# Attention queries with features on partitions, and three smaller moves, in a one-core hybrid mLSTM and window-attention layer

## The chip, the cores and the metric

One Trainium2 chip, one core. The metric is the device time of one execution in microseconds. Before the change three runs took 2311.09, 2317.71 and 2320.4 us; the median is 2317.71 us.

## The reference

One layer of a streaming encoder, in fp32, for a prompt of 2048 tokens and a batch of 8 samples with 16 new tokens each (128 tokens). Model width 1024.

```
z  = x @ w_in                      # mLSTM q,k,v,output gate (4 heads x 128), gates, attention q (8x64), k,v (2x64)
hm = mlstm_chunkwise(q, k, v, ...) # matrix memory with a state per head
hm = sigmoid(o) * head_norm(hm)
qa, ka = rope(qa, pos), rope(ka, pos)
ha = window attention(qa, ka, va)  # own chunk of 64 and the two before it, a learned sink per head
x  = LayerNorm(alpha * x + concat(hm, ha) @ w_out)
u  = causal_depthwise_conv(x @ w_up)       # width 3, value | gate, 2 x 2816
y  = LayerNorm(alpha * x + (silu(gate) * value) @ w_down)
```

`rope` turns each head's two halves of 32 features by an angle that depends on the token: the first half becomes x1 cos - x2 sin, the second x2 cos + x1 sin. Results are y for all tokens, the mLSTM states, the last keys and values and the last rows before the convolution.

## The kernel before

Tokens are 17 tiles of 128: tiles 0 to 15 are the prompt, tile 16 the samples. There are three dense stages, all done as a Winograd form of Strassen's scheme with seven products (numbered 1 to 7) in place of eight: the input projection (blocks of four tiles in `IBLOCKS`, five column groups g of 512, `i_product`), the up-projection (`f_product`) and the down-projection (`f_downs`). The output projection (`o_block`, `group`) is plain. Every matmul operand is split into a high and a low fp32r part, and each product is three matmuls (high by high, high by low, low by high). `split` makes the parts: ScalarE casts the high one, VectorE subtracts to get the low one.

**Input projection.** `i_dense` goes through a written list of items. Groups 0 and 1 (mLSTM queries and keys) have the weights as stationary operand, so that features come out on partitions; groups 2, 3 and 4 (attention queries, output gate, values) have the tokens as stationary operand, so that tokens come out on partitions. `i_after` empties the three PSUM banks A, B, C after each product: ScalarE copies and VectorE adds, then `i_out` and `i_store` write the result to device memory. For group 2, `i_out` first applies `rope` (four VectorE operations on 128 x 512) and writes tokens x features to `zqa`.

**The two chains.** While the dense stages run, two generators work through the prompt's tiles: `m_chain` (mLSTM) and `a_chain` (window attention; `swa` is one tile). They start when `t_sample` has finished the samples. In `a_chain`, `swa_dma` loads the tile's queries and keys, `swa_load` transposes them on TensorE (four 128 x 128 transposes into the bank `pq`, one into `pk`), `swa_first` splits them. `swa` then computes scores in two halves, exponentials, divisions, transposes the weights and multiplies by the values, and `mix_out` writes the tile's result to `zmix`.

**The planner.** `Chains` interleaves them. TensorE's instructions run in the order in which they are written (a manual schedule); the other engines' order is set by the framework's scheduler from priorities. Each yield of a dense stage is worth 645 planned ns (six matmuls of 256 columns or three of 512); each yield of a chain gives its planned cost, the planned delay until its next step, and how many of the five PSUM banks must be free for it. `weave` lets a chain step in when its time has come and its banks are free by plan (`ask` holds each for 3500 ns or what `HOLDS` says). The step list is thus fixed when the program is written, from these numbers alone. `x_pair` loads the chains' results for the next block of the output projection: `OBLOCKS` are tiles 16, 0, 1; 2 to 5; 6 to 9; 10 to 13; 14 and 15, and in the last round of a block the next block's tiles are asked for with

```
for t in OBLOCKS[b]:
    self.chains.until(t)
```

`until` runs chain steps one after the other, with no dense step between, until the tile is ready.

**Weight sums.** The down-projection needs sums of weight blocks. `d_sums(k, step)` makes them during the last two input blocks and the output projection: step 0 loads two rows of `wdn` into `txy`, step 1 is four VectorE subtractions (L850 to L853), step 2 stores them to `zt`.

**End of the up-projection.** `f_evict` empties the banks; after product 5, ScalarE copies bank B to `ub` and VectorE adds bank C to it (L1906, L1908). In the last eight products of `f_ups`, `d_weights` and `d_tokens` prepare the down-projection's first operands with splits on ScalarE and VectorE.

**The end.** In `f_downs` the last product (3) of the last block is done column by column; the last tile's 512 columns are added (L2116), its statistics taken (L1559 and on), and `norm_last` normalises and stores it.

Of the kernel before, what the change touches and what calls it, by code (L numbers as in the profile page):

```python
# [14 lines left out]
P = 128  # L15
# [47 lines left out]
def _consts():  # L63
# [15 lines left out]
    c["rope"] = rp.reshape(NT, P, 3, half).transpose(1, 0, 2, 3)  # L79
    sel = np.zeros((36, MH), np.float32)  # L80
# [124 lines left out]
class Prog:  # L205
# [90 lines left out]
    def setup(self):  # L296
# [10 lines left out]
        self.zqa = [dp.tile([P, 512], F32, name=f"zqa{t}") for t in range(NT)]  # L307
# [384 lines left out]
    def i_product(self, b, g, s):  # L692
# [5 lines left out]
        for c in range(2):  # L698
            m = slice(c * P, c * P + P)
            o = ps[:, c * HT:(c + 1) * HT]  # L700
            for k in range(4):
                for i, (w, x) in enumerate(((wh, hh), (wh, hl), (wl, hh))):
                    l, r = (w[:, k, m], x[:, k]) if g < 2 else (x[:, k, m], w[:, k])
                    mm(o, l, r, start=s in (1, 7) and c == k == i == 0, stop=k == 3 and i == 2, skip_group_check=True)  # L704
# [38 lines left out]
    def i_store(self, b, g, i, j, ev):  # L743
# [3 lines left out]
        if g < 2:  # L747
            f = 4 * i + 2 * g
            nc.sync.dma_start(self.zqk[b][f:f + 2, :, j * HT:(j + 1) * HT].rearrange("f p m -> p f m"), v)
        else:  # L750
            z = (self.zqa, self.zog, self.zv)[g - 2]
# [3 lines left out]
    def i_out(self, b, g, i, j, src):  # L755
# [3 lines left out]
        if g == 3:  # L759
            nc.scalar.activation(ev, src, AF.Tanh, scale=0.5)  # L760
            nc.vector.tensor_scalar_add(ev, ev, 1.0)
        elif not i:
            nc.scalar.copy(ev, src)
        if g == 2:
            self.rope(ev, IBLOCKS[b][2 * j], 2)
        self.i_store(b, g, i, j, ev)

    def i_after(self, b, g, s):
# [4 lines left out]
        def add(u):  # L773
            if g < 2:
                V.scalar_tensor_tensor(u, C, KSCALE, u, op0=ALU.mult, op1=ALU.add)
            else:
                V.tensor_add(u, C, u)
# [23 lines left out]
    def i_batch(self, g):  # L801
# [5 lines left out]
        if g == 2:  # L807
            nc.scalar.copy(ev, ps)
            self.rope(ev, t, 1)
            nc.sync.dma_start(self.zqa[t], ev)  # L810
# [29 lines left out]
    def d_sums(self, k, step):  # L840
# [7 lines left out]
        if step == 1:  # L848
            l, r = slice(0, 512), slice(512, D)
# [8 lines left out]
    def rope(self, A, t, nt):  # L858
# [3 lines left out]
        B = self.mp.tile([P, 512], F32, name="rb", tag="rb", bufs=1)[:, :n]  # L862
# [366 lines left out]
    def swa_dma(self, t):  # L1229
        nc = self.nc  # L1230
        qa = self.work("qa", [P, 512])
        nc.sync.dma_start(qa, self.zqa[t])
        kv = self.work("kva", [P, 256], bufs=3)
        nc.sync.dma_start(kv, self.zkv[t])
        return qa, kv
# [24 lines left out]
    def swa_first(self, t):  # L1260
        nc = self.nc
        kv, pq, pk = self.swa_load(self.a_load)
        self.a_load = None
# [3 lines left out]
        qh, ql = self.work("qh", [P, 4, P], F32R), self.work("ql", [P, 4, P], F32R)  # L1267
        self.split(qh, ql, pq)
        self.split(self.kh[:, r], self.kl[:, r], pk)
        self.kv[r] = kv  # L1270
        self.a_first = qh, ql
# [918 lines left out]
```

## Time and profile before

| | |
|---|---|
| median of three runs | 2317.71 us |
| the profiled execution | 2321.38 us |
| its span, first to last instruction | 2319.6 us |
| mean granted TensorE clock | 0.995 |
| bytes moved by DMA | 632.39 MB, 273 GB/s |

The page gives each engine's busy time over the span, and what each group of instructions waited for. A row of the windows view names a stretch in us from the start of the span, its length, then busy time and instruction count of TensorE, its weight loads, VectorE, ScalarE and GpSimd (of one line alone where a line is asked for: then TensorE and its weight loads only), the granted TensorE clock, the mean busy share of the DMA engines, and GB/s. A row of the groups view gives line, engine, operation, operands, shape and count, then busy us and mean ns of one, then the idle time before. A row of the timeline gives start and length in us, and in brackets the idle time before it with what ended it.

### The profile page before, as it was taken

The numbers are of one execution on the slowest core, as the hardware profiler recorded it, in microseconds if no ns is written. First come the engines' busy times: TensorE is split into PE (matmuls) and PEld (weight loads), VectorE is DVE, ScalarE is ACT, GpSimd is POOL, SyncE is SP. The second block draws the span as 40 slices with busy tenths as digits, with TensorE's granted clock in tenths as the row PEclk, the third lists the DMA queues.
The fourth block names the chain that finished last, engine by engine and source line by source line (L and its number), as shares of the span: only waits on it lengthen the run. The fifth ranks groups of instructions, "written<-read, shape, count | busy, mean of one in ns | idle before, by whom it ended". The sixth has DMA issues, their size and how long they took to land. (4 is left out here: it accounts for less than half of the span.)

```text
span 2319.6 us, 39851 instructions
## 1 busy us (share of the span) xinstructions
PE 2287.3 (99%) x14293; PEld 2097.9 (90%) x14293; DVE 1818.9 (78%) x3189; ACT 1273.3 (55%) x2409; POOL 267.8 (12%) x477
## 2 busy tenths in 40 slices
PE   8999999999999999999999999999999999999998
PEld 8999989899977778999999999999999978888876
DVE  7777687787688888998788777678766786895987
ACT  5453466776766665555556555556555544444442
POOL 0001000100011112121102000003111200100200
PEclk9999999999999999999999999999999999999999
DMA  7888999989986767788777888888998776756743
GB/s 270 289 304 294 302 311 329 313 300 327 334 279 225 234 210 271 286 327 310 279 293 270 307 306 307 314 269 283 313 297 265 227 286 205 258 176 218 258 153 109
DMA packets 300166, 632.39 MB, mean 273 GB/s; under 512 B 47868, under 2 KB 141120, under 8 KB 299968
## 3 DMA queue, kind: packets, MB, share of 16 engines
q1 hardware_dynamic: 295296, 616.14, 77.5%
q0 software_dynamic: 3520, 10.56, 1.4%
q10 hardware_dynamic: 1152, 3.15, 0.4%
q8 instruction: 113, 1.85, 0.3%
q14 instruction: 85, 0.70, 0.1%
HBM read 458.11 MB, written 171.64 MB: 271 GB/s over the span
## 5 line engine op out<-in xcount | busy, mean ns | idle before, releaser
L1877 PE MATMUL dps<-hh,uw 128*128 128x384 f32 (+1 forms) x1848 | 478.1, 328 | 2.6 <-DVE u L1908 2.0
L1877 PE MATMUL fup<-hh,uw 128*128 128x384 f32 (+1 forms) x1848 | 478.1, 328 | 0.3 <-ACT ua L1898 0.2
L1877 PEld LDWEIGHTS dps<-hh,uw 128*128 128x128 f32 x1848 | 329.9, 188 | 3.1 <-DVE u L1908 2.3
L1877 PEld LDWEIGHTS fup<-hh,uw 128*128 128x128 f32 x1848 | 330.0, 188 | 0.8 <-ACT ua L1898 0.5
L1934 DVE SCALAR_TENSOR_TENSOR cc<-u,cw,cc 128x768 f32<-128x768 f32 (+1 forms) x264 | 258.2, 979 | 60.9 <-ACT cc L1932 51.8
L1877 PE MATMUL fup<-hl,uw 128*128 128x384 f32 (+1 forms) x924 | 302.5, 327 | 1.8 <-DVE hl L218 1.8
L1877 PE MATMUL dps<-hl,uw 128*128 128x384 f32 (+1 forms) x924 | 302.3, 327 | 0.0
L704 PE MATMUL dps<-w,oh 128*128 128x256 f32 x1344 | 254.9, 284 | 1.2 <-DMA w<-zws 0.7
L217 ACT CAST uw<-wraw 128x1024 fp32r<-128x1024 f32 x126 | 123.1, 979 | 222.8 <-PE dps L2087 120.1
L218 DVE TENSOR_TENSOR w<-wraw,w 128x1024 fp32r<-128x1024 f32 (+2 forms) x167 | 189.3, 1141 | 50.4 <-ACT w L217 45.7
L704 PEld LDWEIGHTS dps<-w,oh 128*128 128x128 f32 x1344 | 210.6, 188 | 12.7 <-issue 8.1
L217 ACT CAST w<-wraw 128x1024 fp32r<-128x1024 f32 (+2 forms) x167 | 163.2, 984 | 102.9 <-PE dps L704 37.3
L218 DVE TENSOR_TENSOR uw<-wraw,uw 128x1024 fp32r<-128x1024 f32 x126 | 142.5, 1132 | 64.3 <-ACT uw L217 64.3
L704 PE MATMUL dps<-w,ol 128*128 128x256 f32 x672 | 187.9, 280 | 0.0
L704 PE MATMUL dps<-oh,w 128*128 128x256 f32 x896 | 172.5, 287 | 6.2 <-ACT mr L1152 3.4
L1877 PEld LDWEIGHTS fup<-hl,uw 128*128 128x128 f32 x924 | 173.5, 188 | 2.5 <-DVE hl L218 2.4
L2087 PE MATMUL fup<-uw,fu 128*128 128x512 f32 x726 | 174.0, 396 | 0.6 <-DVE uw L218 0.6
L1877 PEld LDWEIGHTS dps<-hl,uw 128*128 128x128 f32 x924 | 173.5, 188 | 0.0
L2087 PEld LDWEIGHTS fup<-uw,fu 128*128 128x128 f32 x726 | 136.3, 188 | 34.0 <-DVE uw L218 1.1
L2087 PE MATMUL dps<-uw,fu 128*128 128x512 f32 x660 | 165.3, 396 | 1.1 <-DVE uw L218 1.1
L1932 ACT ACTIVATE cc<-u,cw 128x768 f32<-128x768 f32 (+1 forms) x132 | 132.2, 1001 | 52.6 <-DVE u L1914 26.7
L704 PEld LDWEIGHTS dps<-oh,w 128*128 128x128 f32 x896 | 143.5, 192 | 12.7 <-issue 4.1
(322 smaller groups left out, 4588.6 us busy)
## 6 DMA issues: line engine op xcount, KB each, us to landing
uw<-zw SPq DMA_DIRECT2D x176, 512.0 KB, 5.2
zw<-uw SPq DMA_DIRECT2D x88, 512.0 KB, 3.6
w<-zws SPq DMA_DIRECT2D x72, 512.0 KB, 6.4
wv<-wup SPq DMA_DIRECT2D x66, 512.0 KB, 4.8
wraw<-wi SPq DMA_DIRECT2D x65, 512.0 KB, 5.3
wraw<-zt SPq DMA_DIRECT2D x60, 512.0 KB, 4.3
wraw<-wdn SPq DMA_DIRECT2D x45, 512.0 KB, 4.2
wraw<-wo SPq DMA_DIRECT2D x40, 512.0 KB, 4.7
```

Of the source, the lines that this page charges most:

```text
L217: nc.scalar.copy(hi, src)
L218: nc.vector.tensor_sub(lo, src, hi.bitcast(F32))
L704: mm(o, l, r, start=s in (1, 7) and c == k == i == 0, stop=k == 3 and i == 2, skip_group_check=True)
L1877: mm(ps, l[:, k], r[:, k], start=s in (1, 7) and k == 0 and i == 0, stop=k == 3 and i == 2, skip_group_check=True)
L1932: S.activation(c[:, v], u[:, 2:2 + n], AF.Identity, bias=w[3], scale=w[2])
L1934: V.scalar_tensor_tensor(c[:, v], u[:, i:i + n], w[i], c[:, v], op0=ALU.mult, op1=ALU.add)
L2087: mm(ps, l[:, k, c], r[:, k], start=s in (1, 4, 7) and u == 0 and k == 0 and i == 0, stop=u == nu - 1 and k == n - 1 and i == 2, skip_grou ...
```

## The change

Four parts.

1. Group 2 of the input projection takes the weights as stationary operand too, so the prompt's queries come out with features on partitions and go to `zq[t]` without rotation. `swa_dma` loads a tile's queries (`qa`), a second copy with the two halves of 32 partitions swapped (`qb`, four DMAs of 32 partitions into the buffer of tag `ql`), and cosine and sine tables (`qcs`). The new `swa_queries` rotates with two multiplications and an addition on VectorE and splits; `swa_keys` keeps the one transpose of the keys. Queries are made one value step later than the keys. Planned costs, delays and bank demands of `swa` change with it. The samples' queries go the old way.
2. Step 1 of `d_sums` is queued on VectorE behind the operation that last emptied a bank (`emptied`), with `issue_after`.
3. At the end of the up-projection the preparation of the down-projection is moved: some of it earlier, and one weight unit and one token unit behind the addition of product 5 (`u4_add`). Four weight units instead of five are made before the down-projection begins.
4. The last tile's last product is done in two halves of 256 columns in two banks; the sum and the statistics of the first half run while the second is computed.

```diff
@@ i_store, i_out
-                    l, r = (w[:, k, m], x[:, k]) if g < 2 else (x[:, k, m], w[:, k])
+                    l, r = (w[:, k, m], x[:, k]) if g <= 2 else (x[:, k, m], w[:, k])
...
+        elif g == 2:
+            for c in range(2):
+                nc.sync.dma_start(self.zq[IBLOCKS[b][2 * j + c]][:, 2 * i:2 * i + 2], v[:, :, c * P:(c + 1) * P])
...
-        if g == 2:
-            self.rope(ev, IBLOCKS[b][2 * j], 2)
+        if not i:
+            self.emptied = z.ins
@@ d_sums
         if step == 1:
+            with self.tc.issue_after(self.emptied):
+                self.d_sums(k, None)
+            return
+        if step is None:
@@ swa_dma
+        qa, qb = self.work("qa", [P, 4, P]), self.work("ql", [P, 4, P], name="qb")
+        nc.sync.dma_start(qa, self.zq[t])
+        cs = self.work("qcs", [P, 2, P])
+        nc.sync.dma_start(cs, self.a["ropeq"][t])
+        for i in range(4):
+            o = (i ^ 1) * 32
+            nc.sync.dma_start(qb[i * 32:i * 32 + 32], self.zq[t][o:o + 32])
@@ swa_queries
+        V.tensor_mul(qa, qa, over(0))
+        V.tensor_mul(qb, qb, over(1))
+        V.tensor_add(qa, qa, qb)
+        qh, ql = self.work("qh", [P, 4, P], F32R), self.work("ql", [P, 4, P], F32R)
+        self.split(qh, ql, qa)
@@ swa
-            self.swa_first(t)
-            yield 550, 4000, 2
+            self.swa_keys(t)
+            self.swa_queries()
+            yield 60, 5500, 2
...
-        yield 0, 4200, 2 + 2 * (self.a_load is not None)
+        yield 0, 4200, 2 + (self.a_load is not None)
...
             if kt == 0 and self.a_load is not None:
-                self.swa_first(t + 1)
-                self.chains.t += 550
-            yield (860 if kt < nk else 0) + (1400 if kt else 0), 0 if kt == nk else 1500 if kt else 3000, 2 * (kt + 1 < nk) + (kt == 0)
+                self.swa_keys(t + 1)
+                self.chains.t += 60
+            if kt == 1 and self.a_load is not None:
+                self.swa_queries()
+            yield (860 if kt < nk else 0) + (1400 if kt else 0), (2500 if nk == 1 else 1500) if kt == nk else 2500 if kt else 3000, 2 * (kt + 1 < nk) + (kt == 0)
@@ f_ups
-            if left in (8, 7, 5, 3, 1):
+            if left in (9, 8, 7):
+                self.d_tokens()
+            if left in (8, 7, 1, 1):
                 self.d_weights()
-            if left in (9, 8, 7, 6):
-                self.d_tokens()
+            if left == 4:
+                with self.tc.issue_after(self.u4_add):
+                    self.d_weights()
+                    self.d_tokens()
@@ f_downs
+                halves = [(slice(i * 256, i * 256 + 256), banks[(role[s][0], 0)[i]][:, :256]) for i in range(2)]
+                S.copy(halves[1][1], banks[role[s][0]][:, 256:])
...
+                for i, (cs, ps) in enumerate(halves):
+                    product(s, 0, range(1, nu), cs, ps)
+                    y = ys[last_tile][:, 512 + i * 256:768 + i * 256]
+                    V.scalar_tensor_tensor(y, y, ALPHA, ps, op0=ALU.mult, op1=ALU.add)
+                    V.bn_stats(st[:, 2 + i], y)
+                self.norm_last(ys[last_tile], *ln2, a["y"][last_tile], st)
```

More of the change, by code (lines that the diff above doesn't have):

```diff
@@ L306, in setup @@
         self.zog = [dp.tile([P, 512], F32, name=f"zog{t}") for t in range(NT)]
-        self.zqa = [dp.tile([P, 512], F32, name=f"zqa{t}") for t in range(NT)]
+        self.zq = [dp.tile([P, 4, P], F32, name=f"zq{t}") for t in range(NPT)]
+        self.zqa = dp.tile([P, 512], F32, name="zqa")
         self.zkv = [dp.tile([P, 256], F32, name=f"zkv{t}") for t in range(NT)]
@@ L1258, in a_chain, with swa_keys @@
             self.chains.done["a"] = t
-    def swa_first(self, t):
+    def swa_keys(self, t):
         nc = self.nc
-        kv, pq, pk = self.swa_load(self.a_load)
-        self.a_load = None
+        kv = self.a_load[1]
+        pk = self.bank([P, P], "pk")
+        nc.tensor.transpose(pk, kv[:, :P], self.ident)
         if t == NPT - 1:
@@ L1557, in stats @@
         s = self.wp.tile([P, 2], F32, name="lsc", tag="lsc", bufs=2)
-        for i in range(half, 2):
-            V.bn_stats(st[:, i], y[:, i * 512:(i + 1) * 512])
+        if st.shape[1] == 2:
+            for i in range(half, 2):
+                V.bn_stats(st[:, i], y[:, i * 512:(i + 1) * 512])
         V.bn_aggr(mv, st)
```

61 lines of the change are left out of this document (37 added, 24 removed).

## The prediction

> **What bounds the kernel now.** I read the page first (engine shares, the slices), then the list of what TensorE waits for, then windows that count the dense steps between two tiles of the attention chain, and the timeline around each long wait.
>
> ```profile
> span 2319.6 us, 39851 instructions
> PE 2287.3 (99%) x14293; PEld 2097.9 (90%) x14293; DVE 1818.9 (78%) x3189; ACT 1273.3 (55%) x2409; POOL 267.8 (12%) x477
> PE dps L704 <- ACT mr L1152: 3.4, 1, 3.4
> PE dps L1877 <- DVE u L1908: 2.0, 1, 2.0
> PE ppt L1346 <- ACT sc L1324: 1.5, 1, 1.5
> ```
>
> TensorE is busy for 2287.3 of 2319.6 us, so 32 us is all that the removal of waits could ever give, and beyond that only TensorE work that disappears counts. The three longest single waits in mid-run are the three shown.
>
> That TensorE is busy between 300 and 870 us is the work of the planner: the two latency-bound chains (mLSTM and window attention) are cut into steps and laid between dense steps of the projections. What protects TensorE there is that each chain ends its tiles before `x_pair` asks for them. If a tile isn't ready, `until` lays all missing steps one after the other with no dense matmul between, and since TensorE runs in written order it waits through their latency. So I stepped the planner's own arithmetic (yields, holds, banks) for the kernel before; it gives an order of steps, no times: 31 dense steps per tile in the output projection, and tile 13's attention ending at dense step 823, `x_pair(3)` asking at 832, and the block ending at 844. The trace agrees (one L222 matmul per dense step):
>
> ```profile
> 692.88:727.71 34.83, 13.81 (x31) 6.26 (x31) 0.95 0.79 266
> 794.45:828.16 33.71, 13.06 (x31) 5.82 (x31) 1.00 0.78 258
> 804.00:825.40 21.40, 9.09 (x22) 4.05 (x22) 1.00 0.87 290
> ```
>
> The first two rows run from one key transpose to the next: 31 steps. The third runs from tile 13's last value product to the end of that block: 22 steps, the last 12 of them behind `x_pair(3)`. The slack is about 9 steps, some 6 us. The same count for tile 15 leaves 12 steps.
>
> **Queries with features on partitions: what goes.** Per prompt tile four transposes leave TensorE.
>
> ```profile
> 339.27 0.60 PE L1242 MATMUL pq<-ident,qa 128*128 128x128 f32 x4
> 339.71 0.27 PE L1244 MATMUL pk<-ident,kva 128*128 128x128 f32 x1
> L871 DVE TENSOR_TENSOR zev<-zev,rb 128x512 f32<-128x512 f32 x17 | 11.7, 687 | 0.2
> qa<-zqa SPq DMA_DIRECT2D x17, 256.0 KB, 5.5
> 300.00:400.00 100.00, 95.83 (x793) 90.10 (x792) 77.69 (x246) 66.55 (x182) 6.21 (x11) 0.97 0.96 318
> ```
>
> The four take 0.44 us from their start to the next instruction's, so 16 tiles give 7.0 us. The product itself keeps its count and its 256 moving columns; only the operands' roles swap: 0. VectorE loses the rotation behind the eviction (two half-width and two full operations) and gains three full ones in the chain, at 0.687 us each about even: 0, covered by VectorE's 22% of idle time. The stores keep their number and bytes, in runs half as long. Each tile loads five DMAs more and 384 KB more (tables 128 KB, swapped copy 256 KB): 6 MB of 632 MB, but in a stretch whose DMA share is 0.96. The swapped copy lands in the buffer of `ql`, so its DMAs stand in SP's queue until the tile's scores have been read, and weight loads stand behind them. Bounds: 0 (the loads have some ten planned us to land, and take 5.5) and 6 MB at 318 GB/s, 19 us, if every byte delayed TensorE. The list of waits has one on a DMA inside the run, 0.7 us, so I take 1 us.
>
> **What the new yields do to the plan.** The attention chain's own delays per tile grow from 18.5 to 21.0 planned us (2500 for 1500 and 1500 for 0 in the value steps), its planned costs fall by 0.49 (550 becomes 60). It asks for one bank less, yet falls out of step with the mLSTM chain, which is let in first and holds banks for 3.5 to 5 us. The same arithmetic with the new yields: in the input projection still about 30 planned us per tile; from tile 4 on, 32 to 40. Attention of tile 9 ends at step 750 instead of 699, tile 11 at 828 instead of 761. At step 832 `x_pair(3)` wants tile 13: tile 12 has only its first half of scores. 22 chain steps are then laid without cover: the rest of attention tile 12, all of 13, the first scores of 14, and mLSTM tile 14 from its scores on and most of 15, some 1.85 tiles of each chain. Tile 14 is woven in normally; of tile 15 the last value step is forced at step 896.
>
> ```profile
> 794.45:828.16 33.71, 33.50 (x191) 25.96 (x189) 28.77 (x79) 23.45 (x61) 4.64 (x5) 1.00 0.78 258
> 1894.31 2.77 PE dps L2087 x12
> 820.00:840.00 20.00, 0.97 (x12) 0.77 (x12) 1.00 0.66 209
> L1307 DVE CUSTOM_DVE_ANT_0 sc<-psc,k_mswa 128x256 f32<-128x256 f32 x120 | 44.1, 417 | 13.6 <-PE psc L1303 13.6
> L1318 ACT ACTIVATE sc<-sc,amx 128x256 f32<-128x256 f32 x63 | 31.3, 499 | 30.1 <-DVE amx L1311 28.2 <-DVE lsc L1561 1.8
> L1318 ACT ACTIVATION_READ_ACCUMULATOR sc<-sc,amx 128x1 f32 x63 | 11.8, 187 | 0.0
> L1324 ACT ACTIVATE sc<-sc,asm 128x256 f32<-128x256 f32 x64 | 27.7, 498 | 5.3 <-DVE asm L1322 4.9 <-DVE asm L1321 0.4
> L1347 ACT COPY pth<-ppt 128x512 f32<-128x512 f32 x32 | 17.1, 583 | 11.3 <-PE ppt L1346 11.3
> L217 ACT CAST w<-wraw 128x1024 fp32r<-128x1024 f32 x35 | 36.6, 1045 | 7.3 <-PE dps L224 5.9 <-PE dps L730 0.7 <-PE dps L223 0.4
> ```
>
> TensorE's part first. A period of 33.71 us holds 31 steps of three matmuls of 512 columns at 0.231 us (2.77/12), 21.5 us, so one tile of both chains is 12.2 us of TensorE; 1.85 tiles are 22.5 us, which must be done anyway. Now the elapsed time. One attention tile, bare: half the scores 0.97; four masked maxima 4 x 0.417 = 1.7; eight exponentials 4.0, with the reads of their sums (0.187 each, half of it hidden) 4.7; eight divisions 4.0; four transposes 0.4; four copies 2.3; the last copy 0.6 and value product, an estimate, 0.5: 15.2 us, of which ScalarE has 11.6. Two such tiles less the start of tile 12 (2.7), with the first scores of 14 (1.0), are 28.7 us. To that come mLSTM steps that stand ahead on ScalarE: of its 23.45 us in the period, 4.6 are weight splits (36.6 us in eight tiles), some 1.5 the splits of the mix and 11.6 attention, so 5.7 are mLSTM, 10 us in 1.85 tiles; I take half, 5. The stretch lasts 33.7 us and loses 11 at full clock. Lower bound: ScalarE never idle, (11.6 + 5.7) x 1.85 = 32 us: 10 lost. The upper one is the clock's.
>
> ```profile
> 688.00:691.00 3.00, 1.53 (x9) 1.03 (x7) 3.00 (x11) 0.56 (x2) 0.00 (x0) 1.00 1.06 334
> 691.00:697.00 6.00, 5.86 (x22) 4.58 (x23) 4.97 (x14) 4.17 (x11) 1.59 (x2) 0.72 1.02 360
> 326.00:329.00 3.00, 2.94 (x25) 2.73 (x24) 1.73 (x3) 2.14 (x7) 0.00 (x0) 1.00 0.98 328
> 329.00:332.40 3.40, 0.02 (x1) 0.03 (x1) 3.25 (x15) 1.70 (x5) 0.00 (x0) 0.78 0.72 236
> 332.40:338.00 5.60, 5.60 (x27) 5.60 (x28) 5.60 (x16) 2.60 (x7) 0.22 (x1) 0.53 1.08 314
> ```
>
> After a wait of only 1.5 us the granted clock is 0.72 for six microseconds, after one of 3.4 us it is 0.53 for 5.6 us. A stretch in which TensorE works 22.5 of 34 us with waits of 1 to 8 us should see the clock low for most of it: at 0.6 throughout, 22.5 us become 37, of which roughly half lies on the chain, 7 us more, and the first dense steps behind it lose another 2. So 11 + 7 + 2 = 20 us; bounds 10 and 26 (all 15 on the chain). The Trainium skill, "TensorE: Matmul & The Clock Gate", section "Why this matters for your kernels", asks only that no idle gap exceed about 3 us between bursts; by it most gaps here would cost no clock, and the term would be about 13. The row at 691 speaks against it; it is a rival below.
>
> Two smaller debts: the forced last value step of tile 15, and the operands of the next blocks, whose write, load and split now begin at the forced point, 16 steps (11 us) before they are needed, with about 11 us to do. Bounds 0 and 6; I take 2.
>
> **Weight sums behind the emptied bank.**
>
> ```profile
> 327.27 0.69 DVE L850 TENSOR_TENSOR txy<-txy 128x512 f32<-128x512 f32 x1 [3.32 <-DMA txy<-wdn]
> 330.70 0.17 ACT L1152 ACTIVATE mr<-pnum 128x2 f32<-128x2 f32 x1 [2.56 <-DVE bst L1149]
> 331.73 0.59 ACT L771 ACTIVATE zev<-dps 128x512 f32<-128x512 f32 x1
> 332.38 0.58 PE L704 MATMUL dps<-oh,w 128*128 128x256 f32 x1 [3.44 <-ACT mr L1152]
> ```
>
> VectorE stood 3.3 us for the weight's load, the norm behind it came late, ScalarE stood for the norm, and the copy that empties the bank stood behind that. With the sums queued after the add that reads the bank, that add no longer has the load ahead of it: 3.44 us go. The clock goes with it: 27 matmuls in 5.6 us, where 25 took 2.94 at full clock (3.2 us for 27), so 2.4 us more. Together 5.8. What is late next is ScalarE's own queue. Bounds: 0 (the new phase of the chains makes another such wait) to 6.
>
> **Last up-projection's splits behind its sum.**
>
> ```profile
> 1839.55 0.41 ACT L1905 COPY ub<-dps 128x320 f32<-128x320 f32 x1
> 1841.29 1.22 DVE L218 TENSOR_TENSOR uw<-wraw,uw 128x1024 fp32r<-128x1024 f32 x1
> 1843.23 0.96 DVE L218 TENSOR_TENSOR fu<-r,fu 128x768 fp32r<-128x768 f32 x1
> 1844.37 0.29 DVE L1908 TENSOR_TENSOR u<-dps,ub 128x128 f32<-128x128 f32 x1
> 1844.71 0.41 PE L1877 MATMUL dps<-hh,uw 128*128 128x320 f32 x1 [2.00 <-DVE u L1908]
> ```
>
> The copy was there at 1840.0, the sum ran at 1844.4 behind two splits. They move behind it: 2.0 us. One weight unit fewer is ready at the first down-product; it is made at step 0 and used at step 4, some 17 us on: 0 while that cover holds, about 1 us (a split) without.
>
> **Last result halved.**
>
> ```profile
> 2312.20 0.69 DVE L2116 SCALAR_TENSOR_TENSOR yacc<-yacc,fht 128x512 f32<-128x512 f32 x1 [1.27 <-PE fht L2087]
> 2312.93 0.69 DVE L1559 BATCH_NORM_STATS2 st<-yacc 128x6 f32<-128x512 f32 x1
> ```
>
> Half of each moves under the second half's matmuls: about 0.6 us. Twice as many matmuls of half the width cost the same (0.118 against 0.231). The added copy to a second bank waits for ScalarE while two other tiles' products run: 0, or 1 us if it is late.
>
> **Sum**, on the profiled execution (2319.6 span, 2321.4 us in all): -7.0 - 5.8 - 2.0 - 0.6 + 1 + 20 + 2 = +7.6, so 2329.0. That execution stood 3.7 us above the median of the runs, 2317.7; on the median's scale I forecast 2325. A difference within 0.5%, 11.6 us, is about what a measurement of this kernel can't tell from none.
>
> **Rivals.** (a) Slower: the clock. If it stays near 0.53 over the whole forced stretch and TensorE's part is all on the chain, the term is 26, and with late operands (6) the sum is +17.6: 2335. It decides once the forced stretch lasts over about 44 us. For it: every long wait in the trace drew a low clock. Against: ScalarE bounds the stretch, so much of the slower TensorE work is hidden. (b) Faster: the change without the forced stretch, if ScalarE and VectorE have run ahead or the plan is kept by something I mis-stepped: -14.4, 2303. Against it: the same arithmetic gave the trace's 31 steps. (c) The skill's rule: clock lost only behind the one gap over 3 us, term 13, 2318: no change. (d) The stall of 332 us or its like comes back in the new phase, and weight loads wait behind the swapped copies in SP's queue: 6 to 8 us more than forecast, 2332. That the change doesn't remove the transposes is excluded by the code.
>
> **Chances.** Forecast case (2319 to 2329) 0.35; (a) and (d) together, slower by over 11.6 us, 0.41; (c) and the forecast's low end (2306 to 2319) 0.12; (b) 0.12. So faster 0.12, same 0.47, slower 0.41. The range takes in (a) with 6 us above it and reaches down into (c): 2309 to 2342, leaving out (b) and the far tail of (a). The likeliest case's own range is 2314 to 2333.
>
> **What would show it.** No L1242 on prompt tiles (4 left, the sample's). No wait of 3 us near 330. In the third output block, near 800 to 840 us, some 35 us with no L222 matmul between L1346, L1352, L1303 and L1213, clock below 0.8, TensorE's slice digits down to 5 or 6. If TensorE stays at 9 there, my planner step is wrong and the time is near 2303. If the stretch is there but under 10 us of it is idle, the price is wrong.

## The result and the profile after

The changed kernel takes 2389.32 us (median of 5 runs, 2387.75 to 2392.57); the kernel before, beside it, 2317.71 us (median of 5, 2311.09 to 2320.4). The ratio is 1.0315, with a 95% interval of 1.0296 to 1.0334: slower by 72 us, where 2325 us was forecast and 2309 to 2342 was the range.

The page of the changed kernel: span, engine shares, and the slices of TensorE and of its granted clock.

```profile
span 2389.2 us, 39819 instructions
PE 2309.9 (97%) x14262; PEld 2113.7 (88%) x14262; DVE 1827.5 (76%) x3176; ACT 1276.1 (53%) x2410; POOL 248.1 (10%) x477
PE   8999999899899979999999999999999999999998
PEclk9999999899999989999999999999999999999999
```

TensorE's idle time was 32 us before and is 79 us now, and the clock falls in the eighth and the fifteenth slice (418 to 478 and 836 to 896 us), which were full before. The list of what TensorE waits for between 300 and 950 us (in total, times, longest) has a first line that the kernel before all but lacked (0.7 us there in the whole run):

```profile
PE dps L710 <- DMA w<-zws: 13.4, 11, 3.9
PE pnum L1228 <- DVE asm L1358: 7.4, 1, 7.4
PE ppt L1383 <- ACT sc L1361: 5.5, 2, 4.8
PE pnum L1228 <- DVE dt L1146: 5.2, 1, 5.2
```

`w<-zws` are the stored halves of weights that the input projection loads again in each block. The wait of 3.4 us behind `mr` near 332 us is gone, as forecast; there are now many others.

To see where the time went, both traces are cut at the same dense steps: 400, 500, 640, 820, 840 and 940. A row gives its window, its length, the busy time of TensorE, weight loads, VectorE, ScalarE and GpSimd, and then the granted clock, the DMA share and GB/s. First the kernel before:

```profile
347.91:455.65 107.74, 107.25 (x905) 98.64 (x903) 79.30 (x245) 75.79 (x202) 9.06 (x13) 1.00 0.96 322
455.65:606.22 150.57, 148.32 (x1238) 137.01 (x1237) 115.53 (x350) 106.45 (x278) 10.49 (x17) 1.00 0.93 320
606.22:800.60 194.38, 192.76 (x1156) 154.77 (x1154) 161.16 (x460) 130.12 (x339) 21.83 (x29) 0.99 0.78 259
800.60:822.78 22.18, 22.18 (x133) 17.41 (x132) 20.89 (x53) 14.16 (x39) 3.60 (x4) 1.00 0.80 268
822.78:914.08 91.30, 91.08 (x472) 71.92 (x470) 72.35 (x147) 52.92 (x109) 7.81 (x6) 1.00 0.67 230
```

The changed kernel, the same steps:

```profile
342.57:468.77 126.20, 113.94 (x879) 103.68 (x878) 79.55 (x228) 75.96 (x203) 6.82 (x12) 0.93 0.85 289
468.77:622.43 153.66, 146.50 (x1191) 133.83 (x1190) 113.87 (x336) 100.00 (x256) 10.29 (x17) 1.00 0.91 304
622.43:824.85 202.42, 189.93 (x1082) 153.23 (x1081) 169.10 (x448) 117.36 (x298) 23.37 (x30) 0.97 0.84 274
824.85:885.30 60.45, 46.34 (x283) 33.80 (x282) 42.44 (x146) 39.91 (x121) 6.11 (x7) 0.89 0.50 160
885.30:983.66 98.36, 91.22 (x426) 69.28 (x425) 68.26 (x116) 51.73 (x102) 5.81 (x4) 0.95 0.59 209
```

Window less busy time is what TensorE lost idle; one minus the clock, times the window, is about what it lost to a low clock. The fourth pair of rows is the forced stretch: 22.2 us became 60.5, 14.1 of it idle and 6.6 lost to the clock. The fifth, behind it, lost 7.1 and 4.9. But the first three, ahead of it, lost 31.9 us idle (4.4 before) and some 15 to the clock (2 before): the changed kernel was 5.3 us ahead at step 400 and is 24.3 us behind at step 820. From step 940 to the end both kernels take 1405.5 us. So three places are to be explained, and only the fourth row was in the prediction at its size.

### The profile page after: what moved, and what is told of

It is laid out like the page before. It is cut to its first block, busy times and chain, and to the rows that moved or that the text cites. A ratio compares the mean times of both kernels' runs of the same rounds, so it can differ in the third digit from the quotient of the medians.

```text
span 2389.2 us, 39819 instructions
## 1 busy us (share of the span) xinstructions
PE 2309.9 (97%) x14262; PEld 2113.7 (88%) x14262; DVE 1827.5 (76%) x3176; ACT 1276.1 (53%) x2410; POOL 248.1 (10%) x477
## 4 chain that ended last, share of the span: by engine, by line
PE 82%; DMA 7%; DVE 6%; ACT 2%; issue 2%; SPq 1%; POOL 0%; DVEq 0%; ACTq 0%; POOLq 0%
PE dps L1923 18%; PE fup L1923 18%; PE dps L710 13%; PE fup L2134 7%; PE dps L2134 6%; PE fht L2134 6%; DMA w<-zws 3%; PE dps L226 2%; PE dps L228 2%; PE dps L227 2%; PE dps L736 1%; PE ppo L1389 1%; PE ppt L1383 1%; PE psx L720 1%; DVE w L222 1%
## 5 line engine op out<-in xcount | busy, mean ns | idle before, releaser
L710 PE MATMUL dps<-oh,w 128*128 128x256 f32 x1344 | 259.7, 287 | 7.0 <-DMA w<-zws 2.1
L710 PEld LDWEIGHTS dps<-oh,w 128*128 128x128 f32 x1344 | 212.8, 189 | 16.6 <-issue 5.1
L710 PE MATMUL dps<-w,oh 128*128 128x256 f32 x896 | 179.1, 293 | 18.9 <-DMA w<-zws 12.7
L710 PE MATMUL dps<-ol,w 128*128 128x256 f32 x672 | 189.9, 283 | 0.4 <-DVE ol L572 0.4
L2134 PE MATMUL fup<-uw,fu 128*128 128x512 f32 (+1 forms) x759 | 177.6, 390 | 1.6 <-ACT fht L2142 1.6
L710 PEld LDWEIGHTS dps<-w,oh 128*128 128x128 f32 x896 | 146.3, 195 | 28.4 <-DMA w<-zws 11.4
```

Of the source, the lines that this page charges most:

```text
L2134: mm(ps, l[:, k, c], r[:, k, cs], start=s in (1, 4, 7) and u == 0 and k == 0 and i == 0, stop=u == nu - 1 and k == n - 1 and i == 2, skip_ ...
```

## The experiments

Two theories stood at the start. P: the plan is out of step, and that makes the loss. Q: the query's copies stand in SyncE's queue ahead of weight loads, which then come late. Two more came up on the way: B, the copies' bytes slow the transfers; V, VectorE's products in the chain are too long. (L, in one expectation, stands for Q and B together: the loads are the loss.)

All times are set against the kernel before, measured beside each run on the same chip (medians of 2316 to 2319 us). "Alone" below means one part put into the kernel before.

### Parts and plan, taken apart

**The plan of before in the changed kernel.**

```
-            yield 60, 5500, 2
+            yield 550, 4000, 2
...
-        yield 0, 4200, 2 + (self.a_load is not None)
+        yield 0, 4200, 2 + 2 * (self.a_load is not None)
...
-                self.chains.t += 60
+                self.chains.t += 550
-            yield ..., (2500 if nk == 1 else 1500) if kt == nk else 2500 if kt else 3000, ...
+            yield ..., 0 if kt == nk else 1500 if kt else 3000, ...
```

> The changed kernel with the attention steps' planned lengths, delays and bank demands of the kernel before (the removed bank is still asked for, so that the planner sees the old queue); the query halves are still made from two rotated copies. By the planner's arithmetic the key transposes of tiles 13 to 15 then fall at dense steps 752, 783 and 814 again and nothing is forced at step 832. Theory P (the plan is out of step) says: the 38 us of the forced stretch and the 8 us of the late operands behind it go, 2389 - 46 = 2343, and if the 24 us lost between steps 400 and 820 come from the plan too, 2343 - 24 = about 2319 or less. Theory Q (the query's copies stand in SyncE's queue in front of the weights) says: the 24 us between steps 400 and 820 stay, so 2343 and not below 2335. If the cost lies in neither, 2389 stays.

Measured: 2362.41 us, ratio 1.0189 (1.0169 to 1.0210). The forced stretch is gone and the plan's share is 27 us; 45 us stay, 19 more than the expectation's upper case (2343). Neither theory had room for that; the run with the plan alone, below, shows where most of it comes from.

**The same, with the queries made one step earlier**, together with the keys.

> As the kernel of the plan of before, with the query's three products and their split issued together with the keys, one step earlier, as the kernel before did with its split. Theory P: no forced stretch, so within 10 us of that run (2319 to 2343). Theory Q: the products then stand in VectorE's queue behind the copies' landing (1.7 to 7.0 us in the changed kernel), so the gaps between steps 400 and 820 get larger, not smaller: 5 to 15 us above that run.

Measured: 2358.56 us, 1.0173 (1.0146 to 1.0201), the same within the intervals, where theory Q had expected 5 to 15 us more. That the products stand one step earlier or later in the chain made no difference that shows.

**The plan of the changed kernel in the kernel before**: the edit above the other way round; queries stay as they were.

> The kernel before with nothing but the planned lengths, delays and bank demands of the changed kernel; the query's transposes stay and are not asked for. By the planner's arithmetic the key transposes fall at the changed kernel's dense steps (365 395 425 458 491 538 ... 816 832 832 855), with the forced stretch at step 832. Theory P: slower by the 38 us of the stretch and the 8 us of the late operands, 2318 + 46 = 2364, and if the plan makes the 24 us between steps 400 and 820 as well, 2388. Theory Q: those 24 us are not there, so 2364 at most. If the stretch costs by something else than the plan, 2318.

Measured: 2350.32 us, 1.0137 (1.0118 to 1.0155): +32 us from planned numbers alone, 14 less than both theories had counted (2364). The forced steps fell where the arithmetic put them, at step 832. The rows of its trace for steps 820 to 840 and 840 to 940:

```profile
783.28:843.73 60.45, 47.54 (x291) 34.89 (x290) 39.71 (x141) 38.88 (x118) 5.35 (x7) 0.89 0.46 148
843.73:942.82 99.09, 91.25 (x430) 69.57 (x429) 66.11 (x112) 51.34 (x102) 5.80 (x4) 0.95 0.59 201
```

The stretch lost 12.9 us idle and 6.6 to the clock, the 100 steps behind it 7.8 and 5.0, together 32. From step 360 to 820 it was idle for 10.3 us, the kernel before for 8.5, so what the changed kernel loses between steps 400 and 820 is not the plan's: theory P covers the stretch and what follows, and no more.

What the plan does ahead of step 820 is to put work off. This kernel stood 17.3 us ahead of the kernel before there (783.28 against 800.60), with 118 matmuls fewer since step 360 (3510 against 3628), and the stretch holds 158 more (291 against 133). So the 38 us by which the stretch grew were never its price, though both theories had counted them as that. In the changed kernel the same postponed work hides a part of the other loss: with the plan of before it stands 38.3 us behind at step 820 (838.93), not 24.3. These 14 us are most of the 19 that the first run had too many.

**One expression of the plan**: the changed kernel with only the delays behind the value steps put back.

```
-            yield ..., (2500 if nk == 1 else 1500) if kt == nk else 2500 if kt else 3000, ...
+            yield ..., 0 if kt == nk else 1500 if kt else 3000, ...
```

> The changed kernel with one expression put back: the delays behind the value steps (0 and 1500 for 1500 and 2500). By the planner's arithmetic the keys' transposes then fall at 365 395 423 454 485 528 ... 814 845, the kernel before's pace, and nothing is forced, though the other planned lengths and bank demands are those of the changed kernel. Theory P (these delays alone put the plan out of step): 2389 - 33 = 2356 (2350 to 2363), with no tile forced at step 832. If the missing bank demand or the shorter planned cost is what does it: 2389.

Measured: 2362.35 us, 1.0185 (1.0169 to 1.0201), as with the whole plan of before. Steps 820 to 840 and the 100 behind them run through again:

```profile
836.82:859.00 22.18, 22.18 (x132) 17.39 (x131) 21.47 (x54) 15.04 (x42) 3.24 (x4) 1.00 0.87 283
859.00:950.65 91.65, 91.53 (x467) 71.45 (x466) 74.43 (x150) 52.94 (x109) 8.65 (x6) 1.00 0.66 232
```

Two delays of 1.0 and 1.5 planned us are the whole of the plan's loss in the changed kernel, 27 us.

**The other half of the plan alone**: bank demands and planned lengths of the changed kernel in the kernel before, delays as they were.

> The kernel before with the changed kernel's bank demands and planned lengths, but the delays of before. By the planner's arithmetic only five key transposes move, by two dense steps each (395, 423, 454, 485 for 393, 421, 452, 483), and nothing is forced. Theory P (the delays make the loss of the plan): 2318, within 5 us. If any change of the order costs some 8 us, as the plan of three tiles did: 2323 to 2330.

Measured: 2322.54 us, 1.0024 (1.0011 to 1.0037), about +6: not the loss, but not nothing either.

**Parts 2 to 4 in the kernel before** (weight sums, splits, halved result; queries and plan of before).

> The kernel before with the changed kernel's weight sums behind the emptied bank, the up-projection's last splits behind its sum and the halved last result; queries and plan are those of before. The prediction's terms for these are -5.8, -2.0 and -0.6: 2318 - 8 = 2309 (2303 to 2315). A rival: the sums taken later, or the reordered splits, cost as much as they save: 2318 or more, and then part of the 71 us is theirs.

Measured: 2329.86 us, 1.0049 (1.0030 to 1.0068): +11, not -8. The rival was right, and two runs say which part it is.

**Part 2 alone.**

```
         if step == 1:
+            with self.tc.issue_after(self.emptied):
+                self.d_sums(k, None)
+            return
+        if step is None:
```

> The kernel before with the weight sums behind the emptied bank and nothing else. The prediction's term: 2318 - 5.8 = 2312 (2310 to 2318). If the sums' new place is what makes the kernel with parts 2 to 4 slower by 12 us: 2330, with the first rise between steps 480 and 500 and the second between 600 and 640, where TensorE there waits for `w<-zws` and for the scores' exponentials.

Measured: 2327.41 us, 1.0044 (1.0030 to 1.0058): +10. Its longest wait of that stage, from the timeline, and the windows of the wait and of the time behind it:

```profile
437.65 0.36 PE L704 MATMUL dps<-w,oh 128*128 128x256 f32 x1 [3.38 <-DMA w<-zws]
434.27:437.65 3.38, 0.00 (x1) 0.03 (x1) 0.69 (x1) 3.38 (x8) 0.00 (x0) 1.00 1.02 390
437.65:443.65 6.00, 5.28 (x32) 5.05 (x32) 2.56 (x3) 0.61 (x3) 0.00 (x0) 0.72 1.10 355
```

The wait near 332 us shrank from 3.44 to 0.95 and 1.68 us, and a wait as long as the old one arose 100 us later, on a weight, with a low clock behind it again (0.72 for 6 us; 0.53 for 5.6 behind the old one).

**Parts 3 and 4 alone.**

> The kernel before with the last up-projection's reordered splits and the halved last result, weight sums and queries as before. The prediction's terms: -2.0 and -0.6, so 2317 - 2.6 = 2314 (2311 to 2317). With the 12 us of parts 2 to 4 and the 10 us of part 2 alone, the sum says +2: 2319.

Measured: 2318.48 us, 1.0000 (0.9991 to 1.0009). Two lines of its list of waits from 950 us on tell why: the wait of 2.0 us on `u` is gone, and the down-projection now waits longer for the splits that were pushed back (3.6 us in three waits, 1.7 in two before).

```profile
PE dps L2103 <- DVE uw L222: 2.7, 2, 1.6
PE fup L2103 <- ACT fht L2111: 0.9, 1, 0.9
```

### What the queries cost

Plan +32, part 2 +10, parts 3 and 4 0: of the 72 us about 30 are left for the queries, which were to bring -6.

**The loads alone.** The kernel before, which issues the five loads and never reads them.

```
+        if t < NPT:
+            qb, cs = self.work("ql", [P, 4, P], name="qb"), self.work("qcs", [P, 112])
+            z = self.zqa[t].rearrange("p (a b) -> p a b", a=4)
+            nc.sync.dma_start(cs, self.a["ropeq"][t][:, 0, :112])
+            for i in range(4):
+                o = (i ^ 1) * 32
+                nc.sync.dma_start(qb[i * 32:i * 32 + 32], z[o:o + 32])
```

> The kernel before, which in addition issues the five loads per prompt tile from SyncE's queue, into the buffers of the swapped copy and of a table, and reads them never (the table's load is cut to 56 KB for want of room: 312 of 384 KB per tile); plan and computation are those of before. Theories Q and B both say that the loads alone bring most of the loss of the queries' change (26 to 32 us): 2338 to 2348, with waits for `w<-zws` of over 10 us. If the products on VectorE and their place in the chain are what costs: 2318 to 2323.

Measured: 2339.65 us, 1.0091 (1.0067 to 1.0115): +21, most of the queries' 30. The waits for `w<-zws` are 6.4 us, not the 10 that were expected. The longest wait, 8.1 us, is put down to a VectorE operation which itself waited for the load of `xr`. SyncE had issued that load at 441 us and four weight loads from 444 us on, all behind the copies of 436 us and a store:

```profile
449.75 1.23 DVE L551 TENSOR_TENSOR wraw<-xr 128x1024 f32<-128x1024 f32 x1 [2.49 <-DMA xr<-xq]
451.03 0.55 PE L708 MATMUL dps<-w,oh 128*128 128x256 f32 x1 [8.09 <-DVE wraw L551]
```

**Bytes or places in the queue.** Three variants of the same: 16 columns of each load; the full loads from GpSimd's queue; the small loads into a buffer of their own, for which nobody has to stand.

```
-                nc.sync.dma_start(qb[i * 32:i * 32 + 32], z[o:o + 32])
+                nc.sync.dma_start(qb[i * 32:i * 32 + 32, 0, :16], z[o:o + 32, 0, :16])   # small
+                nc.gpsimd.dma_start(qb[i * 32:i * 32 + 32], z[o:o + 32])                  # GpSimd
+                nc.sync.dma_start(cs[i * 32:i * 32 + 32, 0], z[o:o + 32, 0, :16])         # small, own buffer
```

> The kernel before with the same five idle loads per tile in the same places of SyncE's queue, but cut to 16 columns each (64 bytes per row, 16 KB per tile instead of 312). If the 22 us of the idle loads are their bytes: 2318 to 2323. If they are the places in SyncE's queue (the issues, and the wait of the copies for the buffer that the scores still read): 2335 to 2342.

> The kernel before with the five idle loads per tile (312 KB) issued from GpSimd's queue: nobody waits for them, and SyncE's queue is that of the kernel before. If the bytes are what costs: 2335 to 2342 as from SyncE's queue. If SyncE's queue is: 2318 to 2323. In between (about 2330): both, or GpSimd's own work, 11% busy, comes late behind the loads.

> The kernel before with the five small idle loads per tile (16 KB), all of them into a buffer of their own that nobody reads, so that SyncE's queue never stands for them; only the five issues per tile are left. If the loss of the small loads (about 13 us) is the standing for the buffer that the scores still read (13.9 us in 7 waits of SyncE's queue there): 2318 to 2322. If five more issues per tile are enough to put the weights' loads late: 2327 to 2332.

Measured: small 1.0057 (1.0035 to 1.0078), +13 us; GpSimd's queue 1.0063 (1.0042 to 1.0083), +15; small in an own buffer 1.0031 (1.0014 to 1.0047), +7. All three fall between the cases that were expected. A twentieth of the bytes leaves more than half of the loss, and without the standing about a third. The intervals of full and small loads overlap, and so do those of the small loads with and without the standing: each of these two steps is likely, not shown; both together are clear of the intervals. From GpSimd's queue the full bytes cost nothing where the loss was: in the traces, steps 360 to 940 take 611.5 us, 612.9 in the kernel before and 631.8 with the loads in SyncE's queue. What that kernel loses comes behind step 940: 11.2 us in its trace, 6.5 of them after the last result (last section).

How a place in the queue costs is to be seen around 425 to 440 us. SyncE's queue in the kernel before:

```profile
424.52 0.80 SPq L753 DMA_DIRECT2D zog<-zev  x2
425.36 0.46 SPq L537 DMA_DIRECT2D xr<-xq  x1
426.24 0.80 SPq L483 DMA_DIRECT2D w<-zws  x2
429.83 0.80 SPq L753 DMA_DIRECT2D zog<-zev  x2
430.72 0.92 SPq L483 DMA_DIRECT2D w<-zws  x2
```

With the small loads, then TensorE's wait there, and one line of the waits of SyncE's queue:

```profile
424.99 2.13 SPq L1245 DMA_DIRECT2D qb<-zqa  x3
427.75 0.81 SPq L757 DMA_DIRECT2D zog<-zev  x2
428.91 1.76 SPq L541 DMA_DIRECT2D xr<-xq  x4
434.06 0.80 SPq L757 DMA_DIRECT2D zog<-zev  x2
434.96 1.87 SPq L487 DMA_DIRECT2D w<-zws  x4
440.03 0.55 PE L708 MATMUL dps<-w,oh 128*128 128x256 f32 x1 [5.60 <-DMA w<-zws]
SPq L1245 <- PE psc L1314: 13.9, 7, 4.9
```

In the kernel before a pair of weight loads slips in between two stores. Here the copies hold the queue, the next loads gather behind them, the store behind those waits for its eviction, and the weights come last, all four at 435 us. In the changed kernel, some 30 us earlier, come three copies, a load and two stores (left out here), and then the weights, on which TensorE waits:

```profile
402.76 2.88 SPq L1259 DMA_DIRECT2D qb<-zq  x3
407.16 2.68 SPq L489 DMA_DIRECT2D w<-zws  x2
416.79 0.80 PE L710 MATMUL dps<-w,oh 128*128 128x256 f32 x2 [2.04 <-DMA w<-zws]
```

The copies are not all of it: at 427.24 us the next two weights go out right behind a store for whose eviction the queue had stood for 9 us. The weights take as long as ever: from issue to landing, from the DMA view of 400 to 660 us, before and in the changed kernel,

```profile
w<-zws SPq DMA_DIRECT2D x36, 512.0 KB, 6.2
w<-zws SPq DMA_DIRECT2D x36, 512.0 KB, 6.1
```

while the DMA share falls (0.96 and 0.93 in the first two rows before, 0.85 and 0.91 after). The transfers aren't slower there; the loads are issued late. (In the variants the same median is 6.1 to 7.3 us.)

**The real copies from GpSimd's queue**, in the kernel with early queries.

> The kernel with the plan of before and early queries (2358.6 us), with the table's load and the four loads of the query's swapped copy issued from GpSimd's queue instead of SyncE's; the bytes are the same. There TensorE waited 20.3 us in 11 waits for `w<-zws`, though these loads landed 6.4 us after their issue, as in the kernel before (6.1). Theory Q (those loads are issued late, because SyncE's queue stands behind stores and the copies): these waits fall under 5 us and the clock loss with them, 2358.6 - 25 = 2333 (2325 to 2341). Theory B (the 6 MB more delay the transfers, whoever issues them): 2353 to 2362, with the waits still above 15 us.

Measured: 2374.21 us, 1.0244 (1.0220 to 1.0268), 16 us worse than from SyncE's queue. TensorE's waits for `w<-zws` fell from 20.3 to 6.5 us, as theory Q has it, but its time (2333) is refuted: VectorE now stands for the copies (300 to 760 us; 0.7 us in two waits with SyncE's queue),

```profile
DVE qb L1304 <- DMA qb<-zq: 46.7, 9, 9.0
```

since GpSimd's queue issues them behind its own waits, and the evictions that TensorE needs stand behind that on VectorE. With the weight sums back in their old place it is no better:

> The same with the weight sums back where the kernel before has them. If the 12 us by which the kernel of before with parts 2 to 4 is slower are the sums' new place, this is some 10 us below the run with the copies from GpSimd's queue: with theory Q 2323 or less, with theory B 2348. If those 12 us come from the reordered splits or the halved result, or only from the order in which steps happen to fall, there is no such difference (within 5 us).

Measured: 2381.25 us, 1.0272 (1.0249 to 1.0294). The 10 us that part 2 cost by itself are not there to be had in this order: without it the kernel is no faster (7 us slower, with intervals that overlap). The parts' prices don't add up.

**No copies**: VectorE reads one block of rows and writes its neighbour.

```
+        for i in range(4):
+            o = (i ^ 1) * 32
+            V.tensor_mul(qb[i * 32:i * 32 + 32], qa[o:o + 32], over(1)[o:o + 32])
-        V.tensor_mul(qb, qb, over(1))
```

> The kernel with the plan of before and early queries (2358.6 us) without the four loads of the swapped copy: VectorE makes the swapped product itself, in four products of 32 partitions that read one block of rows and write its neighbour, against a table with its signs exchanged; result and plan stay. SyncE issues four loads and 256 KB less per tile, VectorE has three products of 512 columns more (about 2 us per tile by the 0.687 us of such a product). The idle loads by themselves cost the kernel before 22 us. Theory L (the loads are the loss, four fifths of them gone): 2358.6 - 18 = 2341 (2334 to 2346). Theory V (the longer work of VectorE ahead of the splits is the loss): not faster than 2356.

Measured: 2351.98 us, 1.0142 (1.0125 to 1.0159): between the two theories. The waits for `w<-zws` fell to 8.4 us, but the longer chain of VectorE shows at once in the scores, which waited 4.0 us at this place with the copies:

```profile
321.79 0.47 PE L1340 MATMUL psc<-kringh,qh 64*128 64x128 f32 x2 [7.27 <-ACT qh L221]
```

**No rotation at all**: queries loaded and split, without table, copies and products; sums and plan of before, parts 3 and 4 in.

> The plan and the weight sums of before, parts 3 and 4, and queries with features on partitions, but the queries are not rotated: no table, no copies, no products on VectorE, nothing but the load and the split. What is left of the queries' change is the swap of operands, the stores in runs half as long and the four transposes less. If the rotation in the chain (its loads and products) makes the whole loss: 2318 - 7 = 2311 (2307 to 2316). If the swap, the stores or the missing transposes shift the order against the transfers as well: 2320 or more.

Measured: 2324.89 us, 1.0036 (1.0016 to 1.0056), +8. The rotation in the chain is the larger part of the queries' loss. What remains isn't the gain of 7 either. TensorE's busy time between steps 360 and 940 is 601.6 us (606.9 with parts 3 and 4 alone), so its transposes did leave, and these steps take 2.4 us less (611.6 and 614.0 us), though it idles 2.9 us more. But the kernel reaches step 360 4.4 us later.

### A version to beat both

The kernel before with the changed plan stood 10.9 us ahead at step 400, before its loss. So its plan was tried for three tiles only:

> The kernel before, with the changed kernel's planned lengths, delays and bank demands for the first three attention tiles only. By the planner's arithmetic the key transposes then fall at dense steps 365 395 425 458 491 538 568 ... 783 813 843 and nothing is forced; tile 13 ends at step 822 (832 is the limit). The kernel before with the whole plan stood 10.9 us ahead of the kernel before at step 400 and 8.8 us ahead at step 440, where the wait of 3.4 us at 332 us was gone. If that lead is the plan's and stays: 2317 - 9 = 2308. If each new order only makes its own waits: anywhere between 2310 and 2330.

Measured: 2326.24 us, 1.0038 (1.0024 to 1.0051). The lead was there (9.4 us at step 400) and was lost again by step 640: TensorE idled 8.8 us on the way, in waits of up to 2.7 us (2.7 us in all in the kernel before), and was busy for 4.9 us more, which isn't explained. No kernel of this study is faster than the one before.

## Why the prediction was wrong, point by point

Forecast and result are 64 us apart. By the measured terms below, the queries make 36 of them (about +30, the part that is left over, for a forecast of -6), the weight sums 16, the operands of the next blocks 10 and the up-projection's end 2.

- **Forced stretch, +20: right in size, in its make-up partly by luck.** The step from planned numbers to the trace held: keys at the computed steps, tile 12 forced at step 832, and 40.1 us between two L226 matmuls (the prediction: 33.7 at full clock, some 41 with it):

```profile
838.65:878.72 40.07, 25.96 (x178) 19.52 (x176) 29.10 (x107) 30.07 (x90) 2.17 (x3) 0.83 0.44 138
848.91 0.77 PE L1228 MATMUL pnum<-v,dt 128*128 128x129 f32 x2 [7.42 <-DVE asm L1358]
867.94 0.48 PE L1383 MATMUL ppt<-ident,sc 128*128 128x128 f32 x1 [4.77 <-ACT sc L1361]
```

  14.1 us idle and 6.6 for the clock are 20.7; in the kernel before with this plan it is 19.5. The prediction had 11 idle, 7 for the clock and 2 more for it right behind. ScalarE worked 30.1 us, near the lower bound of 32. The clock was not at 0.6 throughout: 0.83 on average, above the 0.8 that was named, and the stretch was shorter than rival (a)'s 44 us, so that rival did not come about. Its support, "every long wait in the trace drew a low clock", was a misreading: behind the wait of 2.0 us at 1843 us the clock of the kernel before stayed full. In this stretch it fell only around the two waits over 3 us, as the Trainium skill has it ("TensorE: Matmul & The Clock Gate", "Why this matters for your kernels"); rival (c) still gave too low a term, 13, because it counted one such wait, and 11 us of idle time.
- **Operands of the next blocks, +2: mis-sized.** It measured 12 to 13 us (windows behind the stretch, in both kernels with the plan). The bounds, 0 to 6, counted one block's write, load and split. The next matmul waited 1.7 us, and 60 us later the following block's `oh` came late again (2.0 us), the up-projection's first transposes with it; the low clock made 4.9 us of the loss:

```profile
894.78 0.50 PE L226 MATMUL dps<-w,oh 128*128 128x512 f32 x1 [1.68 <-ACT oh L911]
954.48 0.77 PE L226 MATMUL dps<-w,oh 128*128 128x512 f32 x1 [1.99 <-ACT oh L911]
```

- **DMA and SyncE, +1: the step that failed most.** The loads alone measured +21, the whole of the queries about +30. The bounds, 0 to 19, came from bytes over bandwidth, and the value from a list of waits in which weight loads were hardly ever late. Bytes alone were the wrong measure: the stage lives on weight loads issued just early enough, and the text had said that they would stand behind the copies without pricing it. Rival (d) named this, at 6 to 8 us.
- **Products in the chain, 0: wrong.** VectorE's 22% of idle time was taken for cover. The idle time is an average; in front of the scores VectorE is the path. In the changed kernel the scores wait 3.0 us for the queries' split near 313 us, and 7.3 us with the swap on VectorE; the run without rotation points the same way. How much of the 30 us is loads and how much products isn't settled, since the parts don't add.
- **Weight sums, -5.8 (0 to -6): wrong in sign.** The stall went, but alone the part costs 10 us. The prediction excluded a loss; it named "ScalarE's own queue" as next, and what came next was the weights.
- **Up-projection's end, -2.0: the wait went, the gain didn't.** At the down-projection's first product (1847 us) parts 3 and 4 had won 2.2 us and by 1895 us they had given 2.0 of them back, waiting for the splits that had been pushed behind: the cover that the prediction trusted ("0 while that cover holds, about 1 us without") was not there.
- **Tail, -0.6: right.** From the last matmul to VectorE's last instruction 4.54 us before, 4.05 in every kernel with the halved result.
- **Transposes, -7.0: right as work, somewhat too large.** Without the rotation TensorE's busy time fell by 5.3 us; no version gained time by it.

The sum of what was measured alone, 32 + 10 + 0 + 30, is the 72 us of the result only because the last is the rest; 21 of those 30 have a run of their own.

## What to carry to other kernels

A stage in which TensorE is busy 99% of the time and weights are loaded just ahead of their use has no slack in its queue: count an added DMA by its place in the issuing queue and by what stands behind it, not by its bytes alone. Price a change of order there as well: five small edits of this stage that forced nothing (other demands, three tiles of plan, small loads in an own buffer, part 2, no rotation) cost 6 to 10 us each, and no edit there gained. Why none did, and whether the kernel before merely has a lucky order, was not tested. When work is moved from one stretch to another, its price is the idle time and the clock, not the length of the stretch that takes it in. Where a planner lays out the order by hand-set delays, step it before the change is built: two delays made 27 us, and the arithmetic had the forced step exactly.

## What the runs showed of the hardware

Kernels that issue 80 more loads from GpSimd's queue end later. VectorE's last instruction and the span, with the idle loads from that queue:

```profile
2317.56 1.41 DVE L1558 SCALAR_TENSOR_TENSOR yacc<-yacc,lsc,f_ln_b 128x512 f32<-128x512 f32 x2
span 2328.4 us, 39997 instructions
```

That is 9.4 us from its end at 2319.0 to the end of the program, and 9.4 in both other kernels with such loads, against 2.9 in the kernel before and up to 3.5 in all the rest: some 6 us for work that was done 1400 us earlier. What GpSimd does in that time the trace doesn't show.

A low clock needs no wait of 3 us. In the changed kernel a wait of 1.76 us at 753 us is followed, 1.7 us later, by 3.5 us at half the clock:

```profile
753.02:754.78 1.76, 0.00 (x1) 0.00 (x1) 1.76 (x5) 0.02 (x1) 0.00 (x0) 1.00 0.54 149
754.78:756.50 1.72, 1.58 (x13) 1.24 (x14) 1.72 (x9) 0.95 (x2) 0.00 (x0) 1.00 1.01 262
756.50:760.00 3.50, 3.50 (x10) 2.69 (x9) 3.50 (x16) 0.33 (x2) 0.00 (x0) 0.51 0.99 317
```

The section of the Trainium skill named above asks that no idle gap exceed about 3 us; these rows differ, and the short wait here cost about as much again in clock.

The clock has two values. In all 19 traces it is full or half, never between, and in mid-run each spell of half clock lasts 3.4 us or two or three times that. What the prediction's rows show as 0.72 over six microseconds is one such spell:

```profile
692.69:696.10 3.41, 3.41 (x11) 2.74 (x10) 2.92 (x9) 2.48 (x7) 1.59 (x2) 0.50 1.00 366
```

The length of a short wait doesn't settle whether a spell follows. In the changed kernel waits of 1.57 and 1.61 us at 1939 and 1964 us left the clock full. A wait of 2.64 us near 330 us was followed by 3.4 us of half clock with the full loads in GpSimd's queue, and by none with the small loads in their own buffer.
